# A two-layer hybrid mixer and expert model: norm products, weight scaling and zeroing taken off GpSimd at the passage from mixer to experts

## The chip, the cores and the metric

The kernel runs on one core of one Trainium2 chip, in one launch. The metric is device time of that launch in microseconds: the median of the runs shown. A profile is one execution of the same program; its times are us from the start of its span.

## What is computed

Two layers over 256 latent tokens and 256 context tokens of width 1024, all in float32. Each layer has a mixer (attention, a gated recurrence and a state-space branch, merged and projected by `w_out`) and then a mixture of 64 experts with 8 chosen for each token, plus one shared expert. The part around the change, cut from the reference:

```python
x = layer_norm(DN_ALPHA * x + m[2] * mix, ln1_g[l], ln1_b[l])     # norm1
h2 = (x * (1.0 + m[4]) + m[3]).reshape(B * L, D)
f = swiglu(h2, ws_up, ws_down) + routed_experts(h2, eidx, w, w_up, w_down)
x = layer_norm(DN_ALPHA * x + m[5] * f, ln2_g[l], ln2_b[l])       # norm2
```

`layer_norm` subtracts the mean, divides by the deviation, multiplies by `g` and adds `b`, both of width 1024. In layer 1 (the second, which the kernel calls `last`) only the 256 latent tokens go on to the experts; in layer 0 all 512 do.

## The kernel before

Tokens are held in blocks of 128 rows (`nb` is 4 in layer 0, 2 in layer 1). One function, `sublayer2`, covers the passage that the change touches and all experts after it. Its order of code is the order on each engine's queue; all five queues are in-order. `V`, `S`, `G`, `PE` and `SP` in the code are the engines DVE, ACT, POOL, PE and SyncE. A planner (`Plan`, `Side`) interleaves side work only inside the mixer.

The passage, per block `b`: `w_out` (PE, four column quarters), `norm1` (DVE: multiply by the row `m2`, add the residual, statistics, then two `tensor_scalar` of 128x512 that normalize), `to_h2T` of the block before (PE transposes in two halves, each scaled into `h2T` by ACT), `router` (PE, sigmoid on ACT), and `gain1` of the block before, which multiplies by `ln1_g` and adds `ln1_b`. The scale and shift into `h2T` already hold this gain, so `h2T` reads the block without it and `gain1` is needed only for the later residual. Behind the blocks come `route` of the last blocks (DVE, some 25 short operations that choose the eight experts), `to_h2T` and `router` of the last block, `to_rows` (tokens back to rows; in layer 0 also written to DRAM as `h2d`), `gain1` of the last block, parts of the shared expert (`shared_up`), `sort_experts` (experts ordered by load, on DVE and PE), `places` and the one-hot selection (`one_hot`, `pick_tokens`). Only after the sort are the expert ids known: SP reads them into registers (line 1316) and streams all expert weights but those of the first two, 1 MB a chunk, three chunks an expert, into a ring of 9 slots (11 in layer 1). Then a loop over units `t` of tokens does the experts: in layer 0 each unit's tokens are gathered from `h2d` by an indirect DMA of POOL into one of four buffers `Xb`, and results are scattered; in layer 1 gathering and adding back are matmuls, and the sums stay in PSUM (`acc_ps`).

POOL has this work around the passage: the `pow` of each norm, `gain1`, the zeroing of the four `Xb` (layer 0), the writes to `h2d` and the gathers (layer 0), and in layer 1 the scaling of the shared expert's down weights `shw[2]` by the row `m5`:

```python
G.tensor_tensor(shw[2][:, k, :], shw[2][:, k, :], FR["m5"][0], op=OP.mult)
```

The rows `ln1_g` and `ln1_b` are loaded in the mixer by `before_merge` into the slot `WM`, which in layer 1 is also the last slot of the weight ring. In layer 1 the residual `alpha * x` is scaled on ACT at units 12 and 13 and added into `acc_ps` by a matmul with the identity.

Of the kernel before, what the change touches and what calls it, by code (L numbers as in the profile page):

```python
# [13 lines left out]
AF = mybir.ActivationFunctionType  # L14
# [216 lines left out]
def tile_kernel(ctx: ExitStack, tc: tile.TileContext, A: dict, out: bass.AP):  # L231
# [34 lines left out]
    def slot(l, name, shape, dt=F32, off=0):  # L266
        i = SLOTS[name]
        return view(slots.get(SWAP.get(i, i) if l else i, dt), off, shape)
# [787 lines left out]
    def sublayer2(l, mg, wo, R):  # L1056
# [53 lines left out]
                c = slice(i * 512, (i + 1) * 512)  # L1110
                V.tensor_scalar(x_[:, c], x_[:, c], mv[:, 0:1], mv[:, 2:3], op0=OP.subtract, op1=OP.mult)

        def gain1(b):
            G.tensor_tensor(xr(b), xr(b), R["g1"], op=OP.mult)
            G.tensor_tensor(xr(b), xr(b), R["b1"], op=OP.add)

        def to_h2T(b, both=False):
            s = b // 2
# [125 lines left out]
        def shared_act(b):  # L1244
            shared_up(b, KD - shs[b][1] if b in shs else KD)
            return swiglu_act(shs.pop(b)[0], a=tt[4])
# [56 lines left out]
        def fill(limit=len(chunks)):  # L1303
            while pos[0] < min(limit, len(chunks)):
                if not free:
                    return
                r, i = c = chunks[pos[0]]
                if r >= fixed and not perm:
                    return
                if not last and pos[0] >= len(chunks) - HOLD and free[0] in ("M0", "M1"):  # L1310
                    held.append(free.pop(0))
                    if len(held) == 2:
                        mains[1].start()
                    continue
                if r >= fixed and r not in reg:
                    reg[r] = nc.values_load(perm["row"][0:1, r:r + 1], engines=[mybir.EngineType.SP], min_val=0,
                                            max_val=NE - 1, skip_runtime_bounds_check_because="a permutation of 0..63")
                e = slice(r, r + 1) if r < fixed else bass.ds(reg[r], 1)
                src = A["w_up"][l, e, i] if i < 2 else A["w_down"][l, e]
                place[c] = free.pop(0)  # L1320
                W[c] = slot(l, place[c], (4, 512) if i < 2 else (2, D))
                SP.dma_start(W[c], src.rearrange("o p (k f) -> p (o k) f", k=W[c].shape[1]))
                pos[0] += 1
# [17 lines left out]
        for b in range(nb):  # L1341
            w_out(b, 0)
            if b > 1:
                to_rows(b - 2)
            w_out(b, 1)
            w_out(b, 2)
            if b:
                to_h2T(b - 1)
            if b == 3:
                places(0)  # L1350
            w_out(b, 3)
            if b:
                router(b - 1)
            norm1(b)
            if b:
                gain1(b - 1)
            if b == 2:
                route(0, 2)
            if b + 2 < nb:
                load_x(b + 2)  # L1360
            if not last and b < 2:
                for h in range(2):
                    SP.dma_start(accs[b][:, h * 512:(h + 1) * 512].rearrange("(b p) d -> p b d", p=P),
                                 z[:, None, :].to_broadcast([P, nb + 1, 512]))
        shw.append(load(SHW[2], A["ws_down"][l], (2, D)))
        fill(3 * fixed)


        def sort_experts():
# [93 lines left out]
        yb = None if last else [slot(l, n, (2, D))[:, i, :] for n, i in YBUF]  # L1463
        ysp = [slot(l, "U", (2, D), F32R)[:, i, :] for i in range(2)] if last else None
        for x_ in Xb:
            G.memset(x_, 0.0)
        idx, wcs, toks, acts, ohs = {}, {}, {}, {}, {}
        rows = lambda t: max(c + n for _, _, n, c, _ in units[t])

# [62 lines left out]
        def pick_tokens(t, OH):  # L1532
            ohs[t], OH = OH
            rs = [r for r, _ in pieces(t)]
            step = rs[1] - rs[0] if len(rs) > 1 else 1
            select(t, OH, lambda b: valw[:, rs[0]:rs[-1] + 1:step, b, :], [c for _, c in pieces(t)])
            if not last:
                for si, (_, _, _, c, m) in zip(idx[t], units[t]):
                    gather(si, Xb[t % len(Xb)], slice(c, c + m))
# [160 lines left out]
                                         in_=y, in_offset=None, bounds_check=TL + P - 1, oob_is_err=True,  # L1700
                                         compute_op=OP.add)
        PF = 2 if last else len(Xb) - 1
        g1 = R["g1"][:, :512]
        warm(CHAIN[l][0], banks["sd"][0], g1)
        route(nb - 2, 1)
        to_h2T(nb - 1)
# [1 line left out]
        router(nb - 1)  # L1708
        to_rows(nb - 2, True)
        to_rows(nb - 1, True)  # L1710
        gain1(nb - 1)
        shared_up(0, EARLY_UP[l][0])
        shared_up(0, EARLY_UP[l][1])
        route(nb - 1, 1)
# [7 lines left out]
        if last:  # L1722
            ohs[0] = OH[0]
            turn_x(0, 0)
        pick_tokens(0, OH)
        acts0 = [shared_act(0)]
        if last:
            for k in range(2):
                G.tensor_tensor(shw[2][:, k, :], shw[2][:, k, :], FR["m5"][0], op=OP.mult)
        if not last:  # L1730
            next(srt)
            fill()
# [8 lines left out]
        for t in range(NUN + 1):  # L1741
            OH = None
            if last and t:
                s = spread(t - 1)
                down_split(t - 1)
            if last and t < NUN:
                turn_x(t, 1)
            if last and t and t + PF < NUN:
                OH = one_hot(t + PF)
            if not last and t and t + PF < NUN:  # L1750
                pick_tokens(t + PF, nxt)
            if t < NUN:
                p = bank("mm")
                up(t, p)
                acts[t] = swiglu_act(p, rows(t))
            for _ in srt:
                pass
            if last and t == 0:
                OH = one_hot(PF)
            while first:  # L1760
                i = first.pop(0)
                pick_tokens(i, one_hot(i))
            if todo and t in SHARED_AT[l]:
                b = todo.pop(0)
                shared_down(b, acts0.pop() if acts0 else shared_act(b))
                fill()
            if not last:
                if t == 0:
                    pick_tokens(PF, one_hot(PF))
                if t + 1 + PF < NUN:  # L1770
                    nxt = one_hot(t + 1 + PF)
                if t:
                    down_scatter(t - 1)
                if t + 1 < NUN:
                    turn_x(t + 1, 0)
                    turn_x(t + 1, 1)
                if t < NUN:
                    turn_a(t)
            else:
                if t + 1 < NUN:  # L1780
                    turn_x(t + 1, 0)
                if t and t < NUN:
                    combine(t - 1, s)
                if t < NUN:
                    turn_a(t)
                if OH is not None:
                    pick_tokens(t + PF, OH)
            if t == NUN and not last:
                if len(held) < 2:
                    mains[1].start()  # L1790
                mains[1].split(1, -1)
            if t == OVER[l] + NUN:
                for _ in tables:
                    pass
                overflow(t)
            if t == TABLES:
                tables = overflow_tables()
            if t >= TABLES:
                for _ in range(TSTEP[l]):
                    next(tables, None)  # L1800
            if t == 10:
                fin = fin_rows(l)
            if last and t in (12, 13):
                b = t - 12
                S.activation(xr(b), xr(b), AF.Copy, scale=ALPHA)
                for h in range(2):
                    PE.matmul(acc_ps[2 * b + h], ident, xr(b)[:, h * 512:(h + 1) * 512], start=False, stop=False)
            if not last and t == 0:
                FR["m5"] = [slot(l, "WM", (2, D))[:, i, :] for i in range(2)]
                for s in range(2):  # L1810
                    for _ in mod_row(FR["m5"][s], l, 5, s):
                        pass
            if not last and t == 10:
                free.append("L0")
            if fin and t > 10 and t % 2:
                next(fin, None)

        if last:
# [12 lines left out]
    def before_merge(l):  # L1831
        nst = 1 if l == DEPTH - 1 else 2

        def go():
            mrows = [slot(l, "XB", (2, D))[:, i, :] for i in range(2)]
            m2 = R["m2"] = mrows[:nst]
            if nst == 1:
                FR["m5"] = mrows[1:]

            def rows():  # L1840
                for s in range(nst):
                    yield from mod_row(m2[s], l, 2, s)
                if nst == 1:
                    yield from mod_row(mrows[1], l, 5, 0)
            side.add(rows())
            for _ in range(3):
                yield
            side.drain()
            g1, b1 = [slot(l, "WM", (2, D))[:, i, :] for i in range(2)]
            rows_dma(g1, A["ln1_g"][l])  # L1850
            rows_dma(b1, A["ln1_b"][l])
            R.update(g1=g1, b1=b1)
            yield
        return go
# [241 lines left out]
```

## Time and profile before

| what | value |
|---|---|
| median of 3 runs | 2417.22 us (2413.11 to 2420.92) |
| profiled execution, device time | 2422.18 us |
| its span, first to last instruction | 2420.2 us |
| mean granted TensorE clock | 0.957 of 2.4 GHz |
| busy: PE, DVE, ACT, POOL | 2208.3, 1049.0, 699.1, 477.6 us |
| bytes moved by DMA | 605.24 MB |

The page cuts the span into 40 slices of 60.5 us and gives each engine's busy tenths, the granted clock and the DMA engines' share. Layer 0's mixer fills slices 1 to 11, its experts slices 12 to 23; layer 1's mixer ends in slice 31, and its experts run to the end. Every operation goes through one recording helper, so nearly all rows carry line 149 and have to be told apart by engine, operation, tile and time. In a row of the timeline the second number is the time that the operations of the row took together, `x` counts them, and the bracket gives the idle time ahead of them and what ended it.

### The profile page before, as it was taken

To read this page: it belongs to the slowest core of one execution; us is meant where nothing else is said; L and a number is where in the kernel's file an instruction comes from. 1 tells how busy PE (TensorE), PEld (TensorE's weight loads), DVE (VectorE), ACT (ScalarE), POOL (GpSimd) and SP (SyncE) were. 2 spreads that over 40 slices of the span, in tenths; PEclk is the share of its full clock that TensorE was granted. 3 is DMA by queue.
4 is the path that set the end of the run, shared out by engine and by line. 5 is a ranking of instruction groups with operands and counts; after the bars stand their busy time and mean duration, and the time that the engine had idled before them with its cause. 6 is when DMAs were issued, how large, how long until landed. Compare 5 with 4: busy or idle time off the path is not lost. (4 is left out here: it accounts for less than half of the span.)

```text
span 2420.2 us, 37534 instructions
## 1 busy us (share of the span) xinstructions
PE 2208.3 (91%) x14847; PEld 1388.6 (57%) x14847; DVE 1049.0 (43%) x2315; ACT 699.1 (29%) x1268; POOL 477.6 (20%) x402
## 2 busy tenths in 40 slices
PE   7999999999969999999998849998997899999997
PEld 5778867777844334333333228786995444544553
DVE  4756365533653322332222166666665332333333
ACT  3465355423211111111111124566541111111111
POOL 0223111111232123232332144440212000000000
PEclk8999999999969999999999969999998999999998
DMA  7433333454648999999999942212455789899992
GB/s 293 155 126 108 122 126 124 146 193 142 228 170 295 367 360 347 353 356 350 343 352 354 375 140 89 70 53 101 166 211 221 275 359 421 367 421 420 405 417 84
DMA packets 107218, 605.24 MB, mean 250 GB/s; under 512 B 18216, under 2 KB 18560, under 8 KB 42784
## 3 DMA queue, kind: packets, MB, share of 16 engines
q1 hardware_dynamic: 91608, 560.97, 60.1%
q0 software_dynamic: 13952, 41.57, 7.1%
q8 instruction: 118, 1.93, 0.3%
q14 instruction: 60, 0.49, 0.1%
q10 hardware_dynamic: 1480, 0.27, 0.1%
HBM read 576.54 MB, written 31.06 MB: 251 GB/s over the span
## 5 line engine op out<-in xcount | busy, mean ns | idle before, releaser
L149 PE MATMUL mm<-s,t 128*32 128x512 f32 (+3 forms) x4320 | 668.5, 569 | 29.1 <-DMA s<-in_w_up_dram 26.1
L149 PE MATMUL mm<-s,s 128*128 128x256 f32 (+1 forms) x3488 | 562.8, 320 | 13.4 <-DVE tm L149 8.1
L149 PEld LDWEIGHTS mm<-s,s 128*128 128x128 f32 x3488 | 491.8, 194 | 70.1 <-issue 18.5
L149 PEld LDWEIGHTS mm<-s,t 128*32 128x32 f32 (+2 forms) x4320 | 261.4, 128 | 369.0 <-issue 305.6
L149 DVE TENSOR_TENSOR tm<-tm,mm 128x256 f32<-128x256 f32 (+3 forms) x194 | 85.7, 442 | 572.6 <-ACT tm L149 518.9
L149 ACT ACTIVATE tm<-mm 128x256 f32<-128x256 f32 (+3 forms) x155 | 65.0, 421 | 737.9 <-PE mm L149 720.7
L149 DVE TENSOR_TENSOR s<-s,s 128x1024 fp32r<-128x1024 f32 (+5 forms) x164 | 195.4, 1233 | 47.6 <-ACT s L149 45.4
L149 POOL DMA_INDIRECT acc<-s,si x77 | 110.9, 1441 | 461.7 <-ACT t L149 240.0
L149 PE MATMUL sd<-s,tm 128*32 128x512 f32 (+2 forms) x1112 | 181.1, 612 | 19.3 <-DMA s<-in_w_down_dram 18.0
L149 PE MATMUL sd<-s,s 128*128 128x512 f32 (+4 forms) x768 | 183.3, 455 | 11.5 <-ACT t L149 10.4
L149 ACT ACTIVATE s<-s 128x1024 fp32r<-128x1024 f32 (+4 forms) x170 | 150.5, 939 | 8.9 <-PE sd L149 5.9
L149 PEld LDWEIGHTS sd<-s,s 128*128 128x128 f32 (+2 forms) x768 | 112.1, 187 | 68.0 <-issue 34.4
L149 PEld LDWEIGHTS tr<-t,s 128*128 128x128 f32 x1024 | 125.5, 198 | 43.1 <-issue 42.1
L149 PEld LDWEIGHTS sd<-s,tm 128*32 128x32 f32 (+2 forms) x1112 | 54.6, 120 | 139.2 <-issue 114.1
L149 PE MATMUL tr<-t,s 128*128 128x128 f32 (+1 forms) x1024 | 133.7, 286 | 0.4 <-DVE t L149 0.4
L149 POOL TENSOR_TENSOR s<-s,tm 128x512 f32<-128x512 f32 (+1 forms) x52 | 63.9, 1229 | 319.6 <-ACT tm L149 157.0
L149 PE MATMUL mm<-s,tm 128*32 128x512 f32 (+1 forms) x760 | 108.5, 605 | 12.2 <-ACT tm L149 10.0
L149 ACT ACTIVATE t<-tr 128x512 f32<-128x512 f32 (+6 forms) x115 | 62.0, 544 | 195.6 <-PE tr L149 195.3
L149 PE MATMUL tr<-ident,s 128*128 128x128 f32 (+2 forms) x568 | 84.4, 294 | 35.6 <-DVE s L149 22.9
L149 PEld LDWEIGHTS tr<-ident,s 128*128 128x128 f32 (+2 forms) x568 | 68.1, 151 | 77.2 <-issue 49.8
L149 POOL TENSOR_TENSOR t<-t,mhalf 128x2 f32<-128x2 f32 x1 | 0.7, 707 | 563.7 <-DVE t L149 563.7
L149 ACT ACT_TABLE_LOAD x63 | 80.8, 1283 | 36.4 <-DVE s L149 12.3
(256 smaller groups left out, 2211.8 us busy)
## 6 DMA issues: line engine op xcount, KB each, us to landing
s<-in_w_up_dram SPq DMA_DIRECT2D x256, 1024.0 KB
s<-in_w_down_dram SPq DMA_DIRECT2D x128, 1024.0 KB
s<-in_w_in_dram SPq DMA_DIRECT2D x56, 1024.0 KB
s<-in_w_mod_dram SPq DMA_DIRECT2D x48, 1024.0 KB
t<-in_w_branch_dram SPq DMA_DIRECT2D x32, 256.0 KB
s<-in_w_out_dram SPq DMA_DIRECT2D x8, 1024.0 KB
acc<-t SPq DMA_DIRECT2D x4, 1280.0 KB
s<-in_ws_up_dram SPq DMA_DIRECT2D x4, 1024.0 KB
```

The costliest lines, as they stand in the source:

```text
L149: r = f(*a, **k)
```

## The change

- Layer 0: `gain1` of blocks 0 and 1 stays on POOL. That of block 2 goes to DVE, behind the selection of unit 0; that of block 3 goes to DVE, into unit 0 of the loop.
- Layer 0: the four `Xb` are zeroed by ACT, as copies of a zero tile, where POOL filled them.
- Layer 0: the rows `m5`, which take the slot `WM` over from the norm rows, are built at unit 1 where it was unit 0.
- Layer 1: `gain1` leaves the passage. `late_gain` on DVE at units 10 and 11 does it with the factor alpha folded in, and the two scalings on ACT at units 12 and 13 go.
- Layer 1: `shw[2]` is scaled on DVE at unit 1 where POOL did it ahead of the loop.
- Layer 1: `ln1_g` and `ln1_b` are loaded into the slot `L1`, from the SP queue behind the first experts' weights, where the mixer loaded them into `WM`. The rows of norm2, which use `L1` later, are loaded at unit 17 where it was unit 11.
- The source of the few matmuls that only keep PE busy (`warm`, layer 1) is the row `m2` where it was `ln1_g`.

```diff
-        def gain1(b):
-            G.tensor_tensor(xr(b), xr(b), R["g1"], op=OP.mult)
-            G.tensor_tensor(xr(b), xr(b), R["b1"], op=OP.add)
+        def gain1(b, eng):
+            eng.tensor_tensor(xr(b), xr(b), R["g1"], op=OP.mult)
+            eng.tensor_tensor(xr(b), xr(b), R["b1"], op=OP.add)
+
+        def late_gain(b):
+            V.scalar_tensor_tensor(xr(b), xr(b), ALPHA, FR["g1"], op0=OP.mult, op1=OP.mult)
+            V.scalar_tensor_tensor(xr(b), FR["b1"], ALPHA, xr(b), op0=OP.mult, op1=OP.add)
...
             norm1(b)
-            if b:
-                gain1(b - 1)
+            if b and not last and b < nb - 1:
+                gain1(b - 1, G)
...
         fill(3 * fixed)
+        if last:
+            FR["g1"], FR["b1"] = [slot(l, "L1", (2, D))[:, i, :] for i in range(2)]
+            rows_dma(FR["g1"], A["ln1_g"][l])
+            rows_dma(FR["b1"], A["ln1_b"][l])
...
         for x_ in Xb:
-            G.memset(x_, 0.0)
+            S.activation(fold(x_, (2, 512)), z[:, None, :].to_broadcast([P, 2, 512]), AF.Copy)
...
-        g1 = R["g1"][:, :512]
+        g1 = R["m2"][0][:, :512]
...
         to_rows(nb - 1, True)
-        gain1(nb - 1)
         shared_up(0, EARLY_UP[l][0])
...
         pick_tokens(0, OH)
+        if not last:
+            gain1(nb - 2, V)
         acts0 = [shared_act(0)]
-        if last:
-            for k in range(2):
-                G.tensor_tensor(shw[2][:, k, :], shw[2][:, k, :], FR["m5"][0], op=OP.mult)
...
+            if last and t == 1:
+                for k in range(2):
+                    V.tensor_tensor(shw[2][:, k, :], shw[2][:, k, :], FR["m5"][0], op=OP.mult)
+            if not last and t == 0:
+                gain1(nb - 1, V)
...
-            if t == 10:
+            if t == (15 if last else 10):
                 fin = fin_rows(l)
+            if last and t in (10, 11):
+                late_gain(t - 10)
             if last and t in (12, 13):
                 b = t - 12
-                S.activation(xr(b), xr(b), AF.Copy, scale=ALPHA)
...
-            if not last and t == 0:
+            if not last and t == 1:
                 FR["m5"] = [slot(l, "WM", (2, D))[:, i, :] for i in range(2)]
...
             side.drain()
+            if nst == 1:
+                return
             g1, b1 = [slot(l, "WM", (2, D))[:, i, :] for i in range(2)]
```

Three places in the instruction order matter below. First POOL at the end of layer 0's passage, before; `h2d` is the DRAM copy of the tokens, `ln_mv` the norm's deviation, `s_4810` the block of tokens, `s_5039` and `s_4015` the `Xb`:

```order
L149 DMA h2d_4407<-tm_71 128x512
L149 TENSOR_TENSOR ln_mv<-ln_mv,mhalf 128x1
L149 TENSOR_TENSOR s_4810<-s_4810,s_125 128x1024 x2
L149 MEMSET s_5039 128x1024 x2
L149 MEMSET s_4015 128x1024 x2
L149 DMA h2d_4407<-tm_72 128x512
L149 DMA h2d_4407<-tm_73 128x512
L149 DMA h2d_4407<-tm_71 128x512
```

and now:

```order
L149 DMA h2d_4407<-tm_71 128x512
L149 TENSOR_TENSOR ln_mv<-ln_mv,mhalf 128x1
L149 DMA h2d_4407<-tm_72 128x512
L149 DMA h2d_4407<-tm_73 128x512
L149 DMA h2d_4407<-tm_71 128x512
L149 DMA h2d_4407<-tm_72 128x512
L149 DMA s_5037<-h2d_4407,si 128x1024 x2
```

Between the last norm's `pow` and the writes to `h2d` POOL has nothing left, and the first gather follows the writes directly.

Second ACT at the same place, where `t_4410` is a sigmoid of the router, `s_4405` and `s_4406` are `h2T`, and `s_5037` and `s_4015` the `Xb`; before:

```order
L149 ACTIVATE s_4406<-tr_81,modc_113 128x128 x4
L149 ACTIVATE t_4410<-tr_80 128x64
L149 ACTIVATE s_4405<-tr_81,modc_113 128x128 x4
L149 ACTIVATE s_4406<-tr_80,modc_113 128x128 x4
L149 ACTIVATE t_4410<-tr_81 128x64
```

and now:

```order
L149 ACTIVATE s_4406<-tr_81,modc_113 128x128 x4
L149 ACTIVATE t_4410<-tr_80 128x64
L149 ACTIVATE s_5037<-t_850 128x1024 x2
L149 ACTIVATE s_4015<-t_850 128x1024 x2
L149 ACTIVATE s_4405<-tr_81,modc_113 128x128 x4
L149 ACTIVATE s_4406<-tr_80,modc_113 128x128 x4
L149 ACTIVATE t_4410<-tr_81 128x64
```

The four zeroings stand directly ahead of the two groups that scale the last block into `h2T`.

Third DVE in layer 1's loop at unit 10, where `tkc` and `sprd` belong to the token selection, `t_853` and `s_12081` to the units' results and `s_12976` is a block of tokens; before:

```order
L149 TENSOR_REDUCE wc<-mm_75 32x1
L149 TENSOR_SCALAR tkc<-ixt 128x1
L149 TENSOR_SCALAR sprd<-col_i,tkc 128x256
L149 SCALAR_TENSOR_TENSOR t_853<-mm_74,wc,s_12514 128x512
L149 TENSOR_TENSOR s_12081<-t_853,s_12081 128x512
```

and now:

```order
L149 TENSOR_REDUCE wc<-mm_75 32x1
L149 TENSOR_SCALAR tkc<-ixt 128x1
L149 SCALAR_TENSOR_TENSOR s_12976<-s_12976,s_13134 128x1024
L149 SCALAR_TENSOR_TENSOR s_12976<-s_13134,s_12976 128x1024
L149 TENSOR_SCALAR sprd<-col_i,tkc 128x256
L149 SCALAR_TENSOR_TENSOR t_853<-mm_74,wc,s_12514 128x512
```

The two operations of `late_gain` stand ahead of the operation that empties PSUM for the unit's results.

## Rows read from the trace of the kernel before

**Rows 1.** The page's 40 slices: share of the DMA engines, in tenths.

```profile
DMA  7433333454648999999999942212455789899992
```

**Rows 2.** Timeline of DVE, layer 0's passage: start, us, operations, idle before.

```profile
681.54 8.60 DVE L149 TENSOR_SCALAR s<-s,ln_mv 128x512 f32<-128x512 f32 x2 [0.68 <-POOL ln_mv L149]
...
703.45 1.92 DVE L149 TENSOR_SCALAR t<-t,wsum 128x64 f32<-128x64 f32 x2
...
712.24 0.88 DVE L149 TENSOR_TENSOR t<-t,mm 128x256 f32<-128x256 f32 x2 [4.19 <-ACT t L149]
...
727.64 0.88 DVE L149 TENSOR_TENSOR tm<-tm,mm 128x256 f32<-128x256 f32 x2 [8.39 <-ACT tm L149]
```

**Rows 3.** Timeline of POOL, layer 0's passage.

```profile
681.49 4.82 POOL L149 TENSOR_TENSOR s<-s,s 128x1024 f32<-128x1024 f32 x2
686.24 3.62 POOL L149 MEMSET s<- 128x1024 f32 x4
...
700.37 4.79 POOL L149 TENSOR_TENSOR s<-s,s 128x1024 f32<-128x1024 f32 x2
708.33 1.12 POOL L149 DMA_INDIRECT s<-h2d,si  x1 [3.17 <-DVE si L149]
```

**Rows 4.** Timeline of DVE, layer 1's passage.

```profile
1816.83 1.00 DVE L149 TENSOR_SCALAR s<-s,ln_mv 128x512 f32<-128x512 f32 x2 [0.66 <-POOL ln_mv L149]
...
1829.21 5.04 DVE L149 TENSOR_SCALAR s<-s,ln_mv 128x512 f32<-128x512 f32 x2 [0.66 <-POOL ln_mv L149]
...
1835.76 2.25 DVE L149 TENSOR_TENSOR t<-t,tri 128x64 f32<-128x64 f32 x1
...
1846.11 0.22 DVE L149 TENSOR_TENSOR t<-t,rbias 128x64 f32<-128x64 f32 x1
...
1855.51 0.42 DVE L149 TENSOR_SCALAR t<-t,wsum 128x64 f32<-128x64 f32 x2
```

**Rows 5.** Timeline of PE, layer 0's passage.

```profile
684.15 1.12 PE L149 MATMUL tr<-ident,s 128*128 128x128 f32 x4 [5.17 <-DVE s L149]
690.29 1.09 PE L149 MATMUL tr<-ident,s 128*128 128x128 f32 x4 [5.02 <-DVE trash L149]
...
707.05 0.25 PE L149 MATMUL sd<-idcol,t 128*128 128x2 bf16 x4 [3.09 <-DVE t L149]
...
716.57 1.95 PE L149 MATMUL tr<-ident,s 128*128 128x128 f32 x8
```

**Rows 6.** Timeline of ACT, layer 0's passage.

```profile
685.31 1.50 ACT L149 ACTIVATE s<-tr,modc 128x128 f32<-128x128 f32 x4 [6.07 <-PE tr L149]
```

**Rows 7.** ACT and DVE groups by shape: count, busy us, mean ns, idle before.

```profile
L149 ACT ACTIVATE s<-s 128x1024 f32<-128x1024 f32 x2 | 2.1, 1047 | 0.0
L149 DVE TENSOR_TENSOR s<-s,s 128x1024 f32<-128x1024 f32 x4 | 4.9, 1218 | 0.0
```

**Rows 8.** Timeline of POOL, layer 1's passage.

```profile
1835.53 9.45 POOL L149 TENSOR_TENSOR s<-s,s 128x1024 f32<-128x1024 f32 x4 [1.56 <-PE tr L149]
```

**Rows 9.** Timeline of ACT, layer 1's passage: the last router's sigmoid.

```profile
1839.32 0.22 ACT L149 ACTIVATE t<-tr 128x64 f32<-128x64 f32 x1 [2.34 <-PE tr L149]
```

**Rows 10.** Timeline of PE, layer 1's passage.

```profile
1846.25 0.28 PE L149 MATMUL mm<-ones,t 128*64 128x1 f32 x2 [2.07 <-DVE t L149]
1850.05 0.37 PE L149 MATMUL mm<-ones,t 128*64 128x1 f32 x2 [3.52 <-DVE t L149]
...
1854.21 5.71 PE L149 MATMUL sd<-s,s 128*128 128x512 f32 x8
```

**Rows 11.** One stretch: us; busy PE, PEld, DVE, ACT, POOL; clock; DMA; GB/s.

```profile
1850.00:1855.00 5.00, 3.64 (x15) 2.99 (x16) 2.53 (x14) 0.00 (x0) 0.00 (x0) 0.50 0.07 13
```

**Rows 12.** Waits of the SP queue: who for whom, total, times, longest.

```profile
SPq L1316 <- DVE t L149: 70.2, 2, 38.1
```

**Rows 13.** Timeline of layer 1's loop, one unit: DVE, then PE.

```profile
2050.71 0.75 DVE L149 SCALAR_TENSOR_TENSOR t<-mm,wc,s 128x512 f32<-128x512 f32 x1 [1.16 <-PE mm L149]
2054.18 7.03 PE L149 MATMUL mm<-s,t 128*128 128x512 f32 x16
```

More of the change, by code (lines that the diff above doesn't have):

```diff
@@ L1814, in sublayer2 @@
                 free.append("L0")
-            if fin and t > 10 and t % 2:
+            if fin and t > (15 if last else 10) and t % 2:
                 next(fin, None)
```

## The prediction

> **What bounds the kernel now.** I read the page's slices first. The DMA engines are full in slices 14 to 23 and nearly so, 8 or 9 tenths, in 33 to 39 [rows 1]: those are the two expert stages. Ahead of each the share is lower, 4 to 6 tenths in slices 10 to 12 and 4 to 5 in 29 to 31, because the weights of 62 of the 64 experts cannot be fetched before the experts are sorted. SP's waits say so directly: the load of the sorted ids (line 1316) waits for DVE twice, 70.2 us together, the longer one 38.1 us [rows 12], so the other is 32.1 us. In both layers the sort is the last thing to arrive; whatever delays it delays the whole stage behind it, by the same amount whether that stage is then held by DMA (layer 0) or by PE running unit after unit (layer 1, where a unit's 16 matmuls run 7.03 us without a gap [rows 13]). So I follow the chain that leads to the sort: norm on DVE, transposes on PE, scaling on ACT, router, route on DVE, sort.
>
> On that chain DVE rows stand out. The normalization, two `tensor_scalar` of 128x512, takes 1.00 us where POOL has nothing to do, at 1816.83 [rows 4]. In layer 0 the same two take 8.60 us [rows 2], and exactly then POOL runs `gain1` and the zeroing: 4.82 us from 681.49 and 3.62 us from 686.24, so until 689.9 [rows 3]; DVE ends at 690.14. In layer 1 they take 5.04 us [rows 4] beside another `gain1`. Next `gain1` and the weight scaling, four operations in 9.45 us from 1835.53 [rows 8], meet `route` of block 0: an operation on 64 columns takes 2.25 us there (at 1835.76) [rows 4] where one of that form takes 0.22 (at 1846.11) [rows 4], and there are four such while POOL's four run. I read this as DVE operations of these kinds standing still until POOL's operation is over. The cost of POOL's work is not POOL's time but DVE's standstill, and PE waits for it.
>
> **The change, layer 0.** Step 1, the last norm. Without `gain1` and zeroing on POOL the two operations take 1.00 us and end at 682.54: 7.6 us of DVE. PE's second group of transposes, which waited 5.02 us and began at 690.29 [rows 5], follows the first group; that one can begin at 682.1 (half of 1.00 us after 681.54) and takes 1.12, so the second begins at 683.2, 7.1 us earlier. Then comes ACT. Four zeroings now stand ahead of the two scaling groups. I price one at 1.05 us, a copy of 128x1024 on ACT [rows 7], so 4.2 us, beginning when ACT became idle, at 685.31 less 6.07, or 679.24 [rows 6]: they end at 683.4. The first scaling group could start 1.16 us after its transposes (685.31 against 684.15), at 683.3, so it loses 0.1. Two groups of 1.50 us end at 686.4. Before, the second ended at 690.29 + 1.16 + 1.50, or 692.95. So the router comes **6.5 us** earlier.
>
> Step 2. `gain1` of the last block (POOL, 4.79 us from 700.37 [rows 3]) stops DVE in `places`: 1.92 us (at 703.45) [rows 2] for what takes 0.42 in layer 1 (at 1855.51) [rows 4]. PE waited 3.09 us there for DVE [rows 5], so this **1.5 us** is on the path as well. Layer 0: 8.0 us.
>
> What comes back on DVE: two `gain1`, each two products of 1.22 us [rows 7], 2.4 us. The first stands where DVE was idle for 4.19 us, the second where it was idle for 8.39 us [rows 2]; both waits are for ACT and PE and stay, so I cost them at nothing; without that cover each would cost 2.4. The `m5` rows move by one unit, with the same transposes and copies: nothing.
>
> Against this change stands the first gather. POOL's gather (1.12 us at 708.33 [rows 3]) will now issue while DVE runs the first `gain1`. Its rows are needed at 716.57 [rows 5], 7.1 us after the gather is issued, and both ends shift together. If POOL waited out all of `gain1`, 2.4 us, some 4.7 would remain for the transfer. The Trainium skill, page "SBUF — State Buffer", section "SBUF: two separate sides", says that a DMA issued from POOL has its descriptors written by GpSimd, which a DVE operation in a two-port mode locks out; it gives some 620 ns alone and 3100 ns beside a copy. [...] No row of this case shows a gather beside a DVE operation this long; I take nothing, for the 4.7 us, and keep the delay as a rival.
>
> **The change, layer 1.** The norm falls from 5.04 to 1.00 us, 4.0 less, and `route` of block 0 by four times 2.03, or 8.1: DVE reaches block 1's `route` 12.1 us earlier, at 1834.0 where it was 1846.11. Not all of that reaches the end. PE's second transposes needed the norm's second half, there at 1829.21 + 5.04, or 1834.25. They will follow the first group, at 1829.7 + 1.1 or 1830.8 (the length from layer 0 [rows 5]): 3.5 us earlier. The sigmoid that `route` of block 1 needs, which ended at 1839.54 [rows 9], then ends at 1836.0. That `route` took from 1846.11 to 1850.05, 3.9 us, so it ends at 1839.9. PE itself was free at 1846.25 less 2.07, or 1844.2 [rows 10]; 3.5 earlier is 1840.7. So the count of block 1, at 1850.05 before [rows 10], moves to 1840.7: **9.4 us**. After that PE, not DVE, is what ends last there.
>
> What comes back: the weight scaling on DVE at unit 1, 2.4 us, stands in DVE's wait for that unit's matmuls and sigmoid. Such a wait was 8.39 us in layer 0 [rows 2], and layer 1's units have the same 7 us of matmuls [rows 13]: nothing, and 2.4 without that cover. `late_gain` at units 10 and 11: two operations each, at 1.22 a piece 2.4 us, on DVE ahead of the operation that empties PSUM. That one had 1.16 us of idle before it [rows 13], so it comes 1.3 us late. The bank it empties is needed by the unit's matmuls at 2054.18, and it ended at 2051.46: 2.7 us of margin, so nothing; without the margin 1.3 us twice, or 2.6. The ALPHA copies that go from ACT were off the path: nothing. The norm rows' two loads of 0.5 MB move out of a full DMA stretch to the SP queue ahead of the sorted loads; DMA stands idle there until the sort: nothing, at worst the time of 1 MB at the page's mean of 250 GB/s, 4.2 us by estimate.
>
> **Sum.** 8.0 + 9.4 is 17.4 us. One more term has no sure sign. The eight shared-expert matmuls behind layer 1's sort take 5.71 us, 0.71 each [rows 10]; the granted clock was 0.50, its lower level of 1.2 GHz, just ahead of and into them [rows 11], behind PE waits of 2.07 and 3.52 us. The fast ones, 7.03 us for 16, take 0.44 [rows 13]. With those waits gone they could take 3.5, 2.2 us less. If the clock stays low, nothing. I take 1, near the middle, because the sort still leaves PE with little to do just ahead. Together 18.4 us.
>
> The profiled execution took 2422.18 us with a span of 2420.2, 5 us above the median of 2417.22; I take the difference from both, so 2404 for a like execution and **2399 us** for the median.
>
> **The rivals.** *ACT takes DVE's place* in layer 0. For: the zeroings stand directly ahead of the scaling, with 0.1 us to spare. Against: what they overwrite was last read by block 3's products and norm, just ahead. If each takes twice my price, 4.2 us of the 8.0 go, and the time is 2403.
>
> *The gather waits for DVE.* POOL may stand still for DVE's `gain1` as DVE stood still for POOL's [rows 2, 3]: the gather is then 2.4 us later, and if the transfer needs all of the 7.1 us, PE waits that long: 2401.
>
> *The clock comes back in full*, in both passages: PE gaps of 5.17 and 5.02 us vanish or shrink in layer 0 too [rows 5]. 2.2 us in layer 1 and about as much in layer 0 over the 17.4: 2395.
>
> *The gain does not reach the end.* Weights that the stage gets sooner wait in the ring for slots, and PE and DMA are both near full in layer 1. For: DMA is nearly full in slices 33 to 39 [rows 1]. Against: the waits of 38.1 and 32.1 us [rows 12]. If layer 1 keeps only a third and layer 0 a quarter, some 5 us remain: 2412, within what can be told from no change (0.3%, 7 us).
>
> *SP's queue becomes the bound: slower.* The two norm-row loads stand on SP ahead of all sorted loads of layer 1, and write into a slot that holds a piece of `w_out`. If that slot came free only after the sort, each us beyond would delay all units behind. It decides against the change from 18.4 us after the sort; at 26 us the time is 2425. Against: `w_out` of block 1 is over before its norm at 1829.21 [rows 4].
>
> **How the numbers follow.** Forecast 0.66; ACT 0.09; gather 0.05; clock 0.10; not reaching the end 0.07; slower 0.03. The first four gain more than 0.3%: faster 0.90. The fifth is the same, 0.07; the last slower, 0.03. For the range I go from 2391 (the full clock, 4.4, and 4 us of spread as in the three runs) to 2410 (one of the terms of 4.2 us, one lost cover of 2.4, and the spread). That leaves out the last two cases and some of the edges.
>
> **What would show it.** In the profile after: the last norm of both layers at 1.0 us; four zeroings on ACT ending near 683.5; the router's transposes without the 5.02 us wait; `route` of layer 1's block 0 at 3.9 us; SP's two waits for the sort shorter by about 8 and 9.4; no products on POOL between the last norm of either passage and the loop behind it. The PE waits of 2.07 and 3.52 us become a fraction of one. I am wrong if DVE keeps its 8.60 us, so that POOL was not the cause; if PE waits for ACT behind the zeroings; or if the loops lengthen by what the passages lose.

## The result, and the profile after

The changed kernel takes 2390.77 us, median of 6 runs (2383.72 to 2396.49), against 2414.92 us for the kernel before (median of 6, 2413.11 to 2420.92). The ratio is 0.9895 with a 95% interval of 0.9879 to 0.9911: some 24 to 25 us faster. The forecast of 2399 us had the sign and most of the places right; 2390.77 lies just below its range of 2391 to 2410. Of the 8 us between forecast and result some 6 are the change, which gave 24.2 us in the medians where the sum had 18.4. The other 2.3 are the starting point: the forecast counts from 2417.22 us, the median of the first 3 runs of the kernel before, and over 6 runs that kernel has 2414.92. The profiled execution of after took 2394.08 us with a span of 2392.3, against 2422.18 and 2420.2.

The passage of layer 0, kernel after, timelines of DVE, ACT, POOL and PE (start, us, engine, line, operation, count, idle before and what ended it), to be read against [rows 2, 3, 5, 6]:

```profile
678.78 1.00 DVE L149 TENSOR_SCALAR s<-s,ln_mv 128x512 f32<-128x512 f32 x2 [0.69 <-POOL ln_mv L149]
...
694.05 0.42 DVE L149 TENSOR_SCALAR t<-t,wsum 128x64 f32<-128x64 f32 x2
...
696.98 0.16 DVE L149 SCALAR_TENSOR_TENSOR si<-ixt 128x1 int32<-128x1 f32 x1
697.05 2.48 DVE L149 TENSOR_TENSOR s<-s,s 128x1024 f32<-128x1024 f32 x2
699.63 0.88 DVE L149 TENSOR_TENSOR t<-t,mm 128x256 f32<-128x256 f32 x2
```

```profile
676.35 3.88 ACT L149 ACTIVATE s<-t 128x1024 f32<-128x1024 f32 x4
680.54 2.90 ACT L149 ACTIVATE s<-tr,modc 128x128 f32<-128x128 f32 x8 [0.30 <-PE tr L149]
```

```profile
698.00 1.24 POOL L149 DMA_INDIRECT s<-h2d,si  x1 [6.58 <-DVE si L149]
```

```profile
679.38 1.97 PE L149 MATMUL tr<-ident,s 128*128 128x128 f32 x8 [3.19 <-DVE s L149]
...
696.14 0.25 PE L149 MATMUL sd<-idcol,t 128*128 128x2 bf16 x4 [1.41 <-DVE t L149]
...
696.36 2.82 PE L149 MATMUL mm<-s,s 128*128 128x512 f32 x6
...
705.86 8.51 PE L149 MATMUL mm<-s,t 128*128 128x512 f32 x16
```

The last norm takes 1.00 us where it took 8.60. PE's two groups of transposes have become one row without the 5.02 us wait between them. The zeroing on ACT is over at 680.23, 0.30 us before PE has anything for ACT. The first gather runs inside `gain1` on DVE (697.05 to 699.53) and takes 1.24 us where it took 1.12. It also begins later behind the index that it needs: 0.86 us after `si` is written (697.14), where it was 0.29 (708.33 after 708.04, DVE in the kernel before):

```profile
707.88 0.16 DVE L149 SCALAR_TENSOR_TENSOR si<-ixt 128x1 int32<-128x1 f32 x1
```

The passage of layer 1, kernel after, timelines of DVE and PE, then the waits of the SP queue and the page's DMA slices; they answer [rows 4, 10, 12, 1]:

```profile
1805.49 1.00 DVE L149 TENSOR_SCALAR s<-s,ln_mv 128x512 f32<-128x512 f32 x2 [0.66 <-POOL ln_mv L149]
...
1817.88 1.00 DVE L149 TENSOR_SCALAR s<-s,ln_mv 128x512 f32<-128x512 f32 x2 [0.67 <-POOL ln_mv L149]
...
1820.39 0.23 DVE L149 TENSOR_TENSOR t<-t,tri 128x64 f32<-128x64 f32 x1
```

```profile
1824.88 2.74 PE L149 MATMUL sd<-s,s 128*128 128x512 f32 x6
1827.55 0.39 PE L149 MATMUL mm<-ones,t 128*64 128x1 f32 x4
...
1829.68 0.43 PE L149 MATMUL mm<-t,row_i 64*128 64x64 f32 x2 [1.45 <-DVE t L149]
...
1830.76 5.35 PE L149 MATMUL sd<-s,s 128*128 128x512 f32 x8
...
1865.65 7.03 PE L149 MATMUL mm<-s,t 128*128 128x512 f32 x16
```

```profile
SPq L1321 <- DVE t L149: 47.0, 2, 28.4
```

```profile
DMA  7333333453658999999999942113447689999992
```

The operation on 64 columns that took 2.25 us takes 0.23, and the count of block 1 follows PE's own work without the waits of 2.07 and 3.52 us. SP waits 47.0 us for the two sorts where it waited 70.2.

Where the time came from is best read by stretches between fixed rows, since these can be compared over all kernels below. The unchanged mixer of layer 0 alone moves a profile by several us: block 0's norm, ahead of the first changed instruction, begins anywhere from 622.42 to 629.66 in the 13 profiles of this study. A difference of two profiles from the program's start holds that spread; a stretch inside does not.

| Stretch | before | after | gain |
| --- | --- | --- | --- |
| layer 0: last norm to the first expert's matmuls | 681.54 to 718.35: 36.81 | 678.78 to 705.86: 27.08 | 9.7 |
| layer 0: last norm to layer 1's first norm | 681.54 to 1816.83: 1135.3 | 678.78 to 1805.49: 1126.7 | 8.6 |
| layer 1: first norm to the matmuls behind the sort | 1816.83 to 1854.21: 37.38 | 1805.49 to 1830.76: 25.27 | 12.1 |
| layer 1: first norm to the second expert's matmuls | 1816.83 to 1887.65: 70.82 | 1805.49 to 1865.65: 60.16 | 10.7 |
| layer 1: second expert's matmuls to the end of the span | 1887.65 to 2420.2: 532.6 | 1865.65 to 2392.3: 526.7 | 5.9 |

The ends of these stretches in the kernel before (PE), with six shared-expert matmuls of layer 0 that are used further down:

```profile
707.26 4.52 PE L149 MATMUL mm<-s,s 128*128 128x512 f32 x6
...
718.35 8.79 PE L149 MATMUL mm<-s,t 128*128 128x512 f32 x16
...
1887.65 7.03 PE L149 MATMUL mm<-s,t 128*128 128x512 f32 x16
```

The last line of the table was forecast at nothing. Three pieces of it can be named from rows. In units 12 and 13 PE stood for ACT's scaling by alpha; the first of the two, in the kernel before (PE, then ACT), and the same row of after:

```profile
2117.87 1.98 PE L149 MATMUL sd<-s,ident 128*128 128x512 f32 x4 [1.33 <-ACT s L149]
```

```profile
2116.77 1.05 ACT L149 ACTIVATE s<-s 128x1024 f32<-128x1024 f32 x1
```

```profile
2093.05 1.96 PE L149 MATMUL sd<-s,ident 128*128 128x512 f32 x4
```

From one unit's matmuls to the next, these two units took 20.02 and 20.04 us before (2105.31 to 2125.33 is the first) and take 18.53 and 18.52 now: 3.0 us. The second piece is one group of eight shared-expert matmuls, before and after:

```profile
2004.63 5.40 PE L149 MATMUL sd<-s,t 128*128 128x512 f32 x8 [0.47 <-ACT t L149]
```

```profile
1982.98 3.70 PE L149 MATMUL sd<-s,t 128*128 128x512 f32 x8 [0.47 <-ACT t L149]
```

The granted clock is 0.83 over 2000 to 2010 us before, and 1.00 in both stretches of 10 us from 1980 after: 1.7 us are the lower level of TensorE's clock, with nothing of the change near. The third is one group of an expert's matmuls near the end, before and after (PE):

```profile
2244.43 5.12 PE L149 MATMUL mm<-s,tm 128*32 128x512 f32 x32
```

```profile
2217.98 3.64 PE L149 MATMUL mm<-s,tm 128*32 128x512 f32 x32
```

Again it is the clock: the granted clock is 0.72 over 2244 to 2250 before and 1.00 over 2218 to 2222 after, and the unit takes 20.62 us, then 19.04. The three are together a little more than the 5.9 us of the line. The third is not of the change's making: among the 13 profiles that unit takes 20.6 to 20.7 us in eight and 19.0 in five, and both groups have kernels with the old passages and with the new ones.

### The profile page after: what moved, and what is told of

Read it like the earlier page. It is cut to its first block, busy times and chain, and to the rows that moved or that the text cites. A ratio compares the mean times of both kernels' runs of the same rounds, so it can differ in the third digit from the quotient of the medians.

```text
span 2392.3 us, 37529 instructions
## 1 busy us (share of the span) xinstructions
PE 2197.0 (92%) x14847; PEld 1383.5 (58%) x14847; DVE 1038.9 (43%) x2325; ACT 701.4 (29%) x1270; POOL 450.2 (19%) x388
## 5 line engine op out<-in xcount | busy, mean ns | idle before, releaser
L149 DVE TENSOR_TENSOR s<-s,s 128x1024 fp32r<-128x1024 f32 (+4 forms) x170 | 202.3, 1231 | 46.3 <-ACT s L149 43.8
L149 PE MATMUL sd<-s,s 128*128 128x512 f32 (+4 forms) x768 | 183.5, 454 | 12.2 <-ACT t L149 11.2
L149 ACT ACTIVATE s<-s 128x1024 fp32r<-128x1024 f32 (+3 forms) x168 | 148.4, 937 | 7.4 <-PE sd L149 6.1
L149 PE MATMUL tr<-ident,s 128*128 128x128 f32 (+2 forms) x568 | 83.3, 292 | 24.1 <-DVE s L149 18.4
```

Of the source, the lines that this page charges most:

```text
L149: r = f(*a, **k)
```

## The experiments

**Each layer's part alone.** The first kernel has only what touches layer 0, the second only the rest.

```diff
...
-            if b:
-                gain1(b - 1)
+            if b and (last or b < nb - 1):
+                gain1(b - 1, G)
...
-            G.memset(x_, 0.0)
+            S.activation(fold(x_, (2, 512)), z[:, None, :].to_broadcast([P, 2, 512]), AF.Copy)
...
-        gain1(nb - 1)
+        if last:
+            gain1(nb - 1, G)
...
+        if not last:
+            gain1(nb - 2, V)
         acts0 = [shared_act(0)]
...
+            if not last and t == 0:
+                gain1(nb - 1, V)
...
```

> Only layer 0's part of the change: zeroing on ACT, gain1 of the last two blocks on DVE, the m5 rows one unit later; layer 1 is as before. The prediction's two steps in layer 0 give 8.0 us, about 2407 against 2415. The traces of before and after, less the 2.8 us by which they already differ in the untouched mixer, give 8.5 to 9.7 us. If the passage's gain were absorbed in layer 0's DMA-bound stage, less than 4 us would be left.

```diff
...
-            if b:
-                gain1(b - 1)
+            if b and not last:
+                gain1(b - 1, G)
...
-        gain1(nb - 1)
+        if not last:
+            gain1(nb - 1, G)
...
+            if last and t in (10, 11):
+                late_gain(t - 10)
...
-                S.activation(xr(b), xr(b), AF.Copy, scale=ALPHA)
...
```

> Only layer 1's part: gain1 folded into late_gain, weight scaling on DVE at unit 1, own norm rows, no scaling by alpha on ACT; layer 0 is as before. The prediction gives 9.4 plus 1 for the clock, 10.4 us. The theory after the traces adds 3.0 us for PE's two waits for ACT's alpha scaling at units 12 and 13 and about 1 to 2 for the passage: 14 to 16 us. With e1 the two gains should add up to the whole, about 24 us.

Layer 0's part: 2406.70 us (12 runs) against 2413.84, ratio 0.9977 (0.9960 to 0.9994). Layer 1's part: 2397.11 us (6 runs), ratio 0.9935 (0.9912 to 0.9958). The medians fall by 7.1 and 16.7 us, 23.8 together, and the whole change by 24.2; by the ratios it is 5.6 and 15.7 against some 25. So the parts add up as far as the intervals allow. The traces show where, with less spread. From the last norm to the first expert's matmuls layer 0 takes 27.07 us in the first kernel and 36.85 in the second; from layer 1's first norm to the second expert's matmuls it is 67.45 in the first and 60.02 in the second. So layer 0 was forecast about right (8.0), and layer 1 too low (10.4, with nothing for the copies and for the loop).

**The alpha scaling, moved and put back.** In the kernel before ACT's scalings are issued two units earlier; in the kernel after they return to their old place.

```diff
+            if last and t in (10, 11):
+                S.activation(xr(t - 10), xr(t - 10), AF.Copy, scale=ALPHA)
...
-                S.activation(xr(b), xr(b), AF.Copy, scale=ALPHA)
```

> The kernel before, with ACT's two scalings by alpha at units 10 and 11 where they were at 12 and 13; PE's products that read them stay at 12 and 13. The prediction held them to be off the path: 0 us. The theory after the traces, that PE stood 1.33 and 1.34 us for them and lost what follows in the same unit: 2.5 to 3.0 us faster, no wait of PE on ACT ahead of those two rows.

```diff
-            V.scalar_tensor_tensor(xr(b), xr(b), ALPHA, FR["g1"], op0=OP.mult, op1=OP.mult)
-            V.scalar_tensor_tensor(xr(b), FR["b1"], ALPHA, xr(b), op0=OP.mult, op1=OP.add)
+            V.tensor_tensor(xr(b), xr(b), FR["g1"], op=OP.mult)
+            V.tensor_tensor(xr(b), xr(b), FR["b1"], op=OP.add)
...
+                S.activation(xr(b), xr(b), AF.Copy, scale=ALPHA)
```

> The kernel after, with ACT's two scalings by alpha at units 12 and 13 put back (late_gain without the factor). By the prediction's step they are off the path: the time of the kernel after. By the trace theory PE waits 1.33 us for each and the two units take 20.0 us where they take 18.53: 2.5 to 3.0 us slower than after.

Moved: 2408.88 us (12 runs), ratio 0.9987 (0.9972 to 1.0001), which by itself would not tell 3 us from none. Its row in unit 12 does (PE):

```profile
2105.71 1.96 PE L149 MATMUL sd<-s,ident 128*128 128x512 f32 x4
```

No wait, and both units take 18.53 us. Put back: 2394.18 us, ratio 0.9922 (0.9905 to 0.9939), where the kernel after, run again on that chip, has 2389.95 us, ratio 0.9896 (0.9880 to 0.9912). That difference of 4.2 us is in the expected direction, but the intervals overlap; the rows are sharper. The wait is there again (PE), and the units take 20.03 us:

```profile
2085.98 1.98 PE L149 MATMUL sd<-s,ident 128*128 128x512 f32 x4 [1.34 <-ACT s L149]
```

So these copies cost 3.0 us, shown by moving them out of the way and by putting them back.

**The zeroing back on POOL.** The kernel after, with the old MEMSETs; the gains stay on DVE.

```diff
-            S.activation(fold(x_, (2, 512)), z[:, None, :].to_broadcast([P, 2, 512]), AF.Copy)
+            G.memset(x_, 0.0)
```

> The kernel after, with the zeroing back on POOL as four MEMSETs; the gains stay on DVE. If a MEMSET on POOL makes DVE's tensor_scalar stand as a product does, layer 0's last norm takes 3.5 to 4.5 us where it takes 1.00, and the kernel is 2.5 to 3.5 us slower than after. If only products do it, the norm keeps 1.0 us and the time is that of after.

2395.27 us, ratio 0.9928 (0.9907 to 0.9948). POOL, DVE and PE in that kernel:

```profile
679.22 3.62 POOL L149 MEMSET s<- 128x1024 f32 x4
```

```profile
679.30 4.27 DVE L149 TENSOR_SCALAR s<-s,ln_mv 128x512 f32<-128x512 f32 x2 [0.69 <-POOL ln_mv L149]
```

```profile
683.18 1.97 PE L149 MATMUL tr<-ident,s 128*128 128x128 f32 x8 [6.64 <-DVE s L149]
```

A MEMSET, which reads nothing, holds this operation as a product does: 3.27 us more, and the first expert's matmuls come 29.62 us after the norm where it was 27.08. So 2.5 us of the passage's 9.7 hang on the zeroing alone once the gains are off POOL, the other 7.2 on the gains. Whether the whole kernel loses them is not shown. It is 4.5 us slower in the medians, with intervals of the ratios that just overlap; but in the profile, from the last norm to layer 1's first norm, it takes 1126.3 us, within what the kernels with the zeroing on ACT take (1124.5 to 1126.8), and its loss lies in layer 1's loop (530.9 us from the second expert's matmuls to the end, where after has 526.7), which this edit does not touch.

**Products that nobody needs.** The kernel after, with six products of 128x1024 on POOL in layer 1 where `gain1` and the weight scaling stood. They use rows without a reader in the passage. The last two overwrite a piece of an expert's weights behind the sort, so this kernel does not compute the reference's output and serves for its times alone.

```diff
+        def dummy(n):
+            w = slot(l, "WM", (2, D))
+            for i in range(n):
+                G.tensor_tensor(w[:, i % 2, :], R["m2"][0], R["m2"][0], op=OP.mult)
...
+            if b and last:
+                dummy(2)
...
+        if last:
+            dummy(2)
...
         acts0 = [shared_act(0)]
+        if last:
+            dummy(2)
```

> The kernel after, with six products of 128x1024 put on POOL in layer 1, where POOL's gain1 and weight scaling stood before; they read and write rows that nothing in the passage uses. If DVE stands still because POOL works, layer 1's last norm takes 5 us again and route of block 0 about 12, and the first expert's matmuls come some 10 us later; about 3 of these come back because TensorE's low clock then falls elsewhere: 7 to 10 us slower than after. If DVE waited for gain1's results, recorded as busy time, nothing depends on these products: the norm keeps 1.0 us and the time is that of after.

2397.25 us, ratio 0.9926 (0.9905 to 0.9947): 6.5 us above the kernel after in the medians, a little less than the 7 to 10 expected. POOL, then DVE:

```profile
1819.71 7.80 POOL L149 TENSOR_TENSOR s<-s 128x1024 f32<-128x1024 f32 x4
1854.43 3.74 POOL L149 TENSOR_TENSOR s<-s 128x1024 f32<-128x1024 f32 x2 [26.91 <-DMA s<-in_w_up_dram]
```

```profile
1819.78 4.14 DVE L149 TENSOR_SCALAR s<-s,ln_mv 128x512 f32<-128x512 f32 x2 [0.66 <-POOL ln_mv L149]
...
1823.90 1.84 DVE L149 TENSOR_TENSOR t<-t,rbias 128x64 f32<-128x64 f32 x1
1825.78 0.64 DVE L149 MAX8 t<-t 128x8 f32<-128x8 f32 x8
1826.46 1.09 DVE L149 TENSOR_TENSOR gs<-t 128x8 f32<-128x8 f32 x1
1827.58 0.36 DVE L149 TENSOR_TENSOR t<-gs 128x64 f32<-128x64 f32 x2
```

While POOL works (until 1827.51) the norm and two small additions stand; MAX8 between them does not; after 1827.51 everything is back at its short time. No data ties the two engines here, so DVE stands still because POOL works, and not for a dependence recorded as busy time. The sizes in `route` were expected wrong: the last two products waited for a load until 1854.43 and met nothing, and the first four ran one behind the other, so `route` lost some 2.5 us and not 8. The matmuls behind the sort come 31.97 us after layer 1's first norm (25.27 in after, 37.38 before). The Trainium skill, page "SBUF — State Buffer", section "SBUF: two separate sides", says that the port pair shared by VectorE and GpSimd is an exclusive lock, held for a whole instruction; these rows agree. (Each of the two operations of the norm takes 2.11 us here, beside products of 1.95 us each in the mean.)

**The gains that stayed on POOL.** The changed kernel still ran `gain1` of layer 0's blocks 0 and 1 beside norms of 5.1 us. This kernel puts them on DVE at units 0 and 1.

```diff
-            if b and not last and b < nb - 1:
-                gain1(b - 1, G)
...
-            if not last and t == 0:
-                gain1(nb - 1, V)
+            if not last and t < 2:
+                for b in ((nb - 1, 0), (1,))[t]:
+                    gain1(b, V)
```

> The kernel after, with layer 0's two remaining gain1 (blocks 0 and 1) taken off POOL to DVE at units 0 and 1. The norms of blocks 1 and 2 fall from 5.1 to 1.0 us. If PE's waits behind them (3.94 and 1.28 us) are on the path: 4 to 5 us faster than after. If the next block's w_out or the two gains on DVE (2.4 us each) take it: within 1 us of after.

> The kernel e6_no_gain_pool once more, on the chip of the kernel after. If its gain holds: 4 to 6 us faster than after, with the norms of blocks 1 and 2 at 1.0 us and some 5 us less between the first and the last norm of layer 0. If it came from chip or spread: within 1.5 us of after.

2385.97 us, ratio 0.9879 (0.9859 to 0.9900), and again, beside the kernel after, 2387.54 us, ratio 0.9877 (0.9857 to 0.9897). DVE at block 1's norm, first run:

```profile
637.22 1.00 DVE L149 TENSOR_SCALAR s<-s,ln_mv 128x512 f32<-128x512 f32 x2 [0.66 <-POOL ln_mv L149]
```

From block 0's norm to the first expert's matmuls it is 73.31 and 74.78 us, where the kernel after has 79.23 and 78.31. All 11 runs of this kernel against all 11 of after: 4.1 us less in the mean, with an interval of 1.2 to 7.1. Side by side on one chip the medians differ by 2.4 us, between the 4 to 6 us expected if the gain holds and the 1.5 if it was chance. So this kernel is faster than both others, over the changed one by an amount that a single set of runs does not settle.

**The gaps in the sort, filled.** Seven idle matmuls in PE's two gaps of layer 1's passage, alone and with the edit before.

```diff
+            if last:
+                warm(3, banks["sd"][0], g1)
             V.scalar_tensor_tensor(key[:NE], p[:NE, :NE], float(NE), col_i[:NE, :NE], op0=OP.mult, op1=OP.subtract)
...
         acts0 = [shared_act(0)]
+        if last:
+            warm(4, banks["sd"][0], g1)
```

> The kernel after, with seven idle matmuls in PE's two gaps of the passage of layer 1 (three in the 1.45 us inside the sort, four in the 2.05 us ahead of the second selection). If the low clock behind the sort comes from these gaps, the eight shared-expert matmuls fall from 5.35 to some 3.6 us, the first expert's turns and matmuls lose their 1.7 us as well, and the kernel is 2 to 4 us faster than after. If not, it is 0 to 1 us slower.

> The two edits before together on the kernel after. If both terms hold: 6 to 9 us faster than after. If neither: as after.

The kernel after once more, with no edit:

> The kernel after once more, beside the next two on one chip. Expected: a ratio to before of 0.988 to 0.991, as at first, and in the trace the same passage of layer 1 (shared_up at the low clock, about 60 us from the first norm of layer 1 to the second expert's matmuls), so that the length of the passage is a property of the kernel and not of one profile.

Alone: 2390.69 us, ratio 0.9905 (0.9884 to 0.9926), the time of after. With the other edit: 2384.83 us, 0.9875 (0.9851 to 0.9899), the time of that edit. The rows say why. PE with the idle matmuls, then PE in the kernel after, run again without them:

```profile
1825.51 2.84 PE L149 MATMUL sd<-s,ident 128*128 128x512 f32 x6
1828.28 0.43 PE L149 MATMUL mm<-t,row_i 64*128 64x64 f32 x2
...
1829.36 3.65 PE L149 MATMUL sd<-s,s 128*128 128x512 f32 x8
```

```profile
1828.94 0.43 PE L149 MATMUL mm<-t,row_i 64*128 64x64 f32 x2 [1.45 <-DVE t L149]
...
1830.02 3.65 PE L149 MATMUL sd<-s,s 128*128 128x512 f32 x8
```

The eight matmuls fall to 3.65 us as expected. But three idle matmuls take 2.84 us, more than the gap, and make the sort 1.25 us later (4.46 us from the count to the matmuls behind it, where it is 3.21); and the same kernel after, with the gap of 1.45 us, also ran them in 3.65 us this time, where its first profile had 5.35. The expectation that the passage is a property of the kernel fell: from layer 1's first norm to the second expert's matmuls the kernel after took 60.16 us and then 54.17. What differs is the clock: five groups of PE's work account for the whole 6.0 us (they are listed at the end), and no other row changes by more than 0.3. Just ahead of and in the group that follows the first expert, stretches of 5 us (us; busy PE, PEld, DVE, ACT, POOL; granted clock; DMA; GB/s), first profile and second:

```profile
1855.00:1860.00 5.00, 4.23 (x21) 3.27 (x20) 1.79 (x11) 0.87 (x2) 0.00 (x0) 0.55 0.15 64
```

```profile
1851.00:1856.00 5.00, 4.02 (x24) 2.71 (x23) 2.09 (x10) 0.87 (x2) 0.00 (x0) 1.00 0.16 66
```

In the first that group took 5.67 us (from 1858.36), in the second 3.70 (from 1853.59).

## Why the prediction was short

The step that failed is a term of layer 1 that was put at nothing: "The ALPHA copies that go from ACT were off the path". They were on it, and 3.0 us came with their going. Next to it, the sum left out TensorE's clock in layer 0 (1.7 us) and had the right total for layer 1's passage with two wrong parts. With the 3.0 us the forecast and its range would have been 3 us lower, and the result inside; the mechanism of both passages, DVE standing still while POOL works, was right.

**Layer 0, step 1 and step 2: right.** Router and weights came 8.1 us earlier against the last norm (the scaling of weights by `wsum` ended 23.83 us after that norm began, now 15.69; forecast 8.0). The remaining 1.7 of the 9.7 are six shared-expert matmuls behind it that took 4.52 us and take 2.82: the clock (granted 0.76 over 705 to 712 before, 1.00 over 695 to 700 after), which the sum left out for layer 0 and the rival *the clock comes back in full* had. DMA held nothing back for good: over the whole of layer 0 the kernels with the new passage (after twice, and four others: 1124.5 to 1126.8 us from the last norm to layer 1's first) are 9.4 us below those in the mean with the old one (1133.6 to 1137.0, three kernels).

**Layer 1's passage: the mechanism right, its size too low, its end too high.** The count was forecast 9.4 us earlier and came 11.2 earlier (33.22 us after the first norm, now 22.06). The sum took over PE's own work at its old length, but behind the old waits PE ran slowly there: the idle matmul between the transposes and the router (`sd<-s,ident`, two records) took 1.92 us for what takes 1.02, and the granted clock was 0.81 and 0.77 from 1832 to 1840, where all of 1815 to 1831 in after has 1.00. To the matmuls behind the sort it is 12.1 us (37.4 us in the three kernels with the old passage, 25.3 in five with the new one; two others with the new one have 25.9). Then, in most profiles, the low clock falls on the first expert and some of it goes back: to the second expert's matmuls the old passage took 70.8, 67.5 and 67.2 us, the new one 54.2 to 60.2 in seven kernels, mean 58.4. That is 10.0 us against the 10.4 of the sum, with some 3 us of spread either way. That the totals agree is luck: the count was 1.8 us too low, and behind the sort, where the sum took 1 us for a faster clock, five of these seven kernels lose by the clock.

**"The ALPHA copies that go from ACT were off the path: nothing": wrong, 3.0 us.** The prediction gives no row for it and did not ask who waited for these copies. PE's timeline of before has the two rows with 1.33 and 1.34 us behind ACT, in units 12 and 13; the prediction looked at another unit for the whole loop [rows 13].

**The loop behind it: up to 2.5 us more that were not in the sum.** From the second expert's matmuls to the end it is 532.6 and 533.6 us in the two kernels with the copies in place and the old passage, and 526.2 to 530.9, mean 527.6, in six with neither (and without idle work put in): 5.5 us, of which the copies are 3.0. Of the rest 1.7 are the eight matmuls at 2004.63: the unit they stand in takes 31.7 us in three profiles (before, layer 0's part alone, the idle products) and 30.0 in the other ten. All three have PE's longer waits in the passage; but so has the kernel with the scalings moved, and it takes 30.0. What decides the clock there stays open, and the new passages are not needed for it: the kernel with the scalings moved, old passages and all, takes 526.2 us from the second expert's matmuls to the end. So these 2.5 us are not shown to be the change's.

**Costed at nothing, and right.** `late_gain` takes 2.48 us, the operation that empties PSUM follows it without a wait, and unit 10 still takes 17.17 us. The scaling of `shw` (2.35 us) fits, the first `gain1` on DVE used up its cover but not more (699.63 follows 699.53; the matmuls that its cover, the wait of 4.19 us, was for now take 1.7 us less), the second left 5.72 of 8.39. The norm rows' loads cost nothing that the sort's own stretch shows.

**The rivals.** ACT does not take DVE's place: a zeroing costs 0.97 us, and 0.30 us remained. The gather does not wait out DVE's products of 2.48 us: it ends some 0.7 us later behind its index than before, 0.57 at the start and 0.12 in its own time, and PE does not wait for its rows. The same late start stands in all ten kernels with these products on DVE (0.86 to 0.87 us) and in none of the three without (0.28 to 0.29). The section that the prediction cites for this rival (the Trainium skill, page "SBUF — State Buffer", section "SBUF: two separate sides") speaks of a DVE operation in a two-port mode and, under "Who interferes with whom", says that a product of two tensors has no such mode and was not seen to stall a DMA. The rows agree in the main; the 0.7 us stay unexplained. The clock came back in part: 1.7 us in layer 0, and in layer 1 with either sign from one profile to the next. The gain reached the end, and SP's queue did not bind. In sum: 9.4 for layer 0, 10.0 for layer 1's passage and 3.0 for the copies make 22.4 us, and 24.9 with the 2.5 of the loop, against 24 to 25 in the medians and 18.4 in the forecast.

## What to carry to other kernels

An elementwise operation that is off the critical path on GpSimd (POOL) can still be on it through VectorE (DVE): look for VectorE operations whose time is several times that of the same form elsewhere, and see what GpSimd ran just then. Before an operation is called free to remove, ask the engine that consumes its result whether it waited, in each unit where it stands, and not the engine that runs it. Where a wait on the path goes, the matmuls behind it may run at the other clock level; that was worth up to 6 us here, with either sign, so the forecast needs it as a range and the profile needs more than one execution.

## What the runs showed of the chip

- VectorE's standstill beside GpSimd is selective. `tensor_scalar` of 128x512 and additions of 8 and 64 columns stood (4.14, 1.09 and 1.84 us); MAX8 in the midst of them kept its 0.64 us. A MEMSET on GpSimd is enough (4.27 us where it takes 1.00).
- Between two products VectorE gets in, between zeroings it did not: beside the idle products the norm's two operations took 2.11 us each, one product apiece; beside the four zeroings the first took 3.82 us, to the end of the last zeroing, and the second 0.53.
- One kernel, two profiles, one passage: 60.16 and 54.17 us, all of it the clock's level in five groups of matmuls and transposes (5.35, 3.06, 7.70, 2.73 and 5.67 us against 3.65, 2.03, 7.03, 2.05 and 3.70).
- Without any change ahead of it, layer 0's first norm begins between 622.42 and 629.66 us after the start, a spread of 7.2 us; whole runs of one kernel lie 4 to 20 us apart.
